# Reordering the matmul groups of an MLP's second projection in a decoder-layer kernel

## The chip, the core and the metric

The kernel runs on one core of one Trainium2 chip. The metric is the device time of one execution in microseconds (us), the median over several runs. Five engines run from separate instruction queues and meet at semaphores: TensorE (PE; its weight loads are listed as PEld), VectorE (DVE), ScalarE (ACT), GpSimd (POOL) and SyncE (SP), which here issues the DMAs from the chip's memory (HBM). The time before is 1776.33 us, the median of 3 runs (1775.65 to 1777.22).

## The reference

One layer of a decoder with 256 tokens and width 2048. Three mixing branches come first; the change touches only the MLP at the end, whose inner width is 8192:

```python
for l in range(DEPTH):
    ...
    x = x + rmsnorm(merged @ w_out[l], g_post_mix[l])
    h2 = rmsnorm(x, g_pre_mlp[l])
    m = jnp.square(jax.nn.relu(h2 @ w_mlp_in[l])) @ w_mlp_out[l]
    x = x + rmsnorm(m, g_post_mlp[l])
return x
```

All data is float32. `w_mlp_in` is 2048 x 8192, `w_mlp_out` 8192 x 2048.

## The kernel before, in words

**Split operands.** Each float32 operand is split into a high part (a cast to fp32r) and a low part (the operand minus the high part), and a product is three matmuls: high by high, high by low, low by high. For a block of weights of 2 x 128 rows by 512 columns (0.5 MB), SP loads it into a buffer `raw`, ACT casts it to `oh`, and DVE subtracts to get `ol`. Six buffers of each kind are used in rotation (`operand`, `raw`). A `raw` buffer can be loaded again when DVE's subtraction has read it; an `oh`/`ol` pair can be written again when PE has used it.

**Stages of the MLP.** The inner width is cut into eight experts `e` of 1024. `mlp_in(e)` makes the first projection in two halves `u` of 512 columns, eight blocks of weights each; at the end of a half, ACT and DVE move the sums out of PSUM into a tile `relu`, DVE squares the positive part in place, and the result is split into `mh` and `ml` (`gen_relu`). `mlp_out(e - 1)` follows `mlp_in(e)` and adds the expert's part of the second projection. `mlp_out_last` does the last expert.

**The second projection.** The output has 2048 columns. Columns 1024 to 2047 are done plainly: for `c` = 2 and 3, `unit` runs over four blocks of weights ("groups", 12 matmuls of 512 columns each) and accumulates two tokens' tiles in PSUM. Columns 0 to 1023 are done by a scheme of seven products instead of eight (`seven`). Products 6, 4, 5 and 3 take sums of blocks of weights, which DVE adds in the `raw` buffers before the split (`summed`); products 0, 1 and 2 take a block as it is (`bare`, the plain products). Each product has two steps `d` = 0 and 1 of 6 matmuls; at the end of `d` = 1 its PSUM bank is added to an accumulator `acc` by DVE (for expert 0, copied by ACT). Products 6 and 4 share one PSUM tile of two banks, and so do 0 and 1. Some products use sums of the activations, which `gen_sums` makes for the next expert: four half-width DVE instructions on `relu`, and two splits `sh`/`sl`. In the order of the program the four steps of the summed products at `d` = 0 come first, then two groups of the unit for `c` = 2, then the summed products at `d` = 1, then the other two groups; the same follows with the plain products and `c` = 3.

**What sets the order.** The code lists work in a program order; the framework that builds the program then places each engine's instructions in an order of its own. Small steps of other work (`gen_sums`, `gen_relu`) are kept in a list `bg`, from which `tick` takes steps after each group or product. In the build before, the squaring and the split of a half go through this list, for the second half only after `drain`.

In the rows below, `mm` is a PSUM tile, and buffer numbers are left out in the profile (so `ol` stands for all six).

Of the kernel before, what the change touches and what calls it, by code (L numbers as in the profile page):

```python
# [10 lines left out]
F32 = mybir.dt.float32  # L11
# [3 lines left out]
ALU = mybir.AluOpType  # L15
AX = mybir.AxisListType

P = 128
D = 2048
S = 256  # L20
NT = S // P
# [12 lines left out]
KG = 2  # L34
# [6 lines left out]
def tile_trunk(ctx: ExitStack, tc, a):  # L41
# [48 lines left out]
    def nm(s):  # L90
        cnt[0] += 1
        return f"{s}_{cnt[0]}"
# [14 lines left out]
    def bank(name):  # L107
        return pbp.tile([P, 512], F32, tag="bp", name=nm(name))
# [52 lines left out]
    bg = []  # L161
# [11 lines left out]
    def drain():  # L173
        while bg:
            pump(1)
# [56 lines left out]
    def unit(act, nk, src, c0, r0=0, order=None, split=False, post=None, ws=None, load=None):  # L232

        if split:
            ps = [bank("mm") for _ in range(2)]
        else:
            both = pmm.tile([P, 1024], F32, tag="mm", name=nm("mm"))  # L240
            ps = [both[:, 0:512], both[:, 512:1024]]
        if order is None:
            order = [(g, None) for g in range(nk // KG)]
        ws = ws or {}
        for i, (g, tt) in enumerate(order):
            k0 = g * KG
            if g not in ws:
                ws[g] = load(src, r0 + k0, c0) if load else load_w(src, r0 + k0, KG, c0)
            wh, wl = ws[g]
            for j in range(KG):  # L250
                kt = k0 + j
                ah, al = act(kt)
                for t in range(NT) if tt is None else (tt,):
                    o = ps[t]
                    st, sl = ah[:, t * P:(t + 1) * P], al[:, t * P:(t + 1) * P]
                    T.matmul(o, st, wh[:, j, :], start=kt == 0, stop=False)
                    T.matmul(o, st, wl[:, j, :], start=False, stop=False)
                    T.matmul(o, sl, wh[:, j, :], start=False, stop=kt == nk - 1)
            tick()
            if post is not None and i + 1 in post:  # L260
                post[i + 1](ps)
        return ps if split else both
# [56 lines left out]
    def act_of(tiles):  # L319
        return lambda kt: (tiles[kt // 4][0][:, kt % 4, :], tiles[kt // 4][1][:, kt % 4, :])  # L320
# [1134 lines left out]
    def raw(src, k0, c0):  # L1455
        w = raws.pop(0)
        raws.append(w)
        nc.sync.dma_start(w, src[k0 * P:(k0 + KG) * P, c0:c0 + 512].rearrange("(k p) n -> p k n", p=P))
        return w
# [24 lines left out]
            yield  # L1484

    def mlp_in(e):
        mt, rs, steps = [], [], []
        for u in range(2):
            c0 = e * 1024 + u * 512
            hi, lo = g4("mh", (P, 4, S), F32R), g4("ml", (P, 4, S), F32R)  # L1490
            r = g4("relu", (P, 4, S))
            if e == 0 and u == 0:
                rt = g4("relut")
                ps = unit(h2act, KT, a["w_mlp_in"][0], c0, order=first, ws=ahead)
                wide_ring()
                A.activation(rt, ps, AF.Relu)
                V.scalar_tensor_tensor(out=rt, in0=ps, scalar=0.0, in1=rt, op0=ALU.max, op1=ALU.mult)
                bg.append(gen_turn(rt, r, hi, lo))
            else:
                if u == 1:  # L1500
                    ps = [bank("mm") for _ in range(4)]
                else:
                    ps = []
                    for _ in range(2):
                        both = pmm.tile([P, 1024], F32, tag="mm", name=nm("mm"))
                        ps.extend((both[:, 0:512], both[:, 512:1024]))
                unit_stacked(h2B, KT, a["w_mlp_in"][0], c0, ps, load_in,
                             {g: ahead[8 + g] for g in range(2)} if e == 0 else {})
                for c in range(4):
                    A.copy(r[:, c, :], ps[c][:, S:2 * S])  # L1510
                    V.tensor_tensor(out=r[:, c, :], in0=ps[c][:, 0:S], in1=r[:, c, :], op=ALU.add)
                steps.append(gen_relu(r, hi, lo))
                if u == 0 or e == 0:
                    bg.append(steps.pop())
            mt.append((hi, lo))
            rs.append(r)
        return mt, rs, steps

    def gen_relu(r, hi, lo):
        V.scalar_tensor_tensor(out=r, in0=r, scalar=0.0, in1=r, op0=ALU.max, op1=ALU.mult)  # L1520
        A.copy(hi, r)
        yield
        V.tensor_tensor(out=lo, in0=r, in1=hi.bitcast(F32), op=ALU.subtract)
        yield

    def gen_sums(rs, ops):

# [20 lines left out]
    def add_w(out, in0, in1):  # L1548
        V.tensor_tensor(out=out, in0=in0, in1=in1, op=ALU.add)
# [3 lines left out]
    def seven(e, mt, ops):  # L1553

        if e == 0:
            for i in range(4):
                t = g4("acc", (P, 2, 512))  # L1560
                accs.extend((t[:, 0, :], t[:, 1, :]))
        acts = [halves_of(mt[0], 0), halves_of(mt[1], 0), halves_of(ops[1], 0), halves_of(mt[1], 1),
                halves_of(ops[0], 1), halves_of(ops[1], 1), halves_of(ops[0], 0)]
        ps = [None] * 7

        def product(i, w, d):
            wh, wl = split_w(w, KG, home=operand)
            for j in range(KG):
                ah, al = [z[:, d * KG + j, :] for z in acts[i]]
                begin, end = d == 0 and j == 0, d == 1 and j == KG - 1  # L1570
                T.matmul(ps[i], ah, wh[:, j, :], start=begin, stop=False)
                T.matmul(ps[i], ah, wl[:, j, :], start=False, stop=False)
                T.matmul(ps[i], al, wh[:, j, :], start=False, stop=end)
            if d == 1:
                if e == 0:
                    A.copy(accs[i], ps[i])
                else:
                    V.tensor_tensor(out=accs[i], in0=ps[i], in1=accs[i], op=ALU.add)
            tick(0.5)

        def summed(d):
            k1 = e * 8 + d * KG
            k2 = k1 + 4
            if d == 0:
                both = pmm.tile([P, 1024], F32, tag="mm", name=nm("mm"))
                ps[6], ps[4] = both[:, 0:512], both[:, 512:1024]
                ps[5], ps[3] = bank("mm"), bank("mm")
            w12, w22, w11, w21 = raw(w_mo, k1, 512), raw(w_mo, k2, 512), raw(w_mo, k1, 0), raw(w_mo, k2, 0)
            add_w(w22, w22, w12)
            add_w(w12, w12, w11)  # L1590
            product(6, w22, d)
            add_w(w11, w22, w11)
            product(4, w12, d)
            add_w(w21, w11, w21)
            product(5, w11, d)
            product(3, w21, d)

        def bare(d):
            k1 = e * 8 + d * KG
            k2 = k1 + 4  # L1600
            if d == 0:
                both = pmm.tile([P, 1024], F32, tag="mm", name=nm("mm"))
                ps[0], ps[1] = both[:, 0:512], both[:, 512:1024]
                ps[2] = bank("mm")
            product(0, raw(w_mo, k1, 0), d)
            product(1, raw(w_mo, k2, 0), d)
            product(2, raw(w_mo, k2, 512), d)

        return summed, bare

    def joined():
# [37 lines left out]

    def mlp_out(e, mt, ops, after):  # L1650
        summed, bare = seven(e, mt, ops)
        for c, part in ((2, summed), (3, bare)):
            if c == 3 and after is not None:
                bg.append(after)
            part(0)
            ps = unit(act_of(mt), 8, w_mo, c * 512, e * 8, split=True, load=load_in, post={2: lambda ps: part(1)})
            if e == 0:
                y_ = g4("yacc", (P, NT, 512))
                yacc[c] = [y_[:, t, :] for t in range(NT)]
            for t in range(NT):  # L1660
                if e == 0:
                    A.copy(yacc[c][t], ps[t])
                else:
                    V.tensor_tensor(out=yacc[c][t], in0=ps[t], in1=yacc[c][t], op=ALU.add)

    def mlp_out_last(e, mt):
        yacc[0:2] = joined()
# [16 lines left out]
                mlp_evac(c, t, ps[t])  # L1684
                gain(c, t)

    prev, rs, _ = mlp_in(0)
    bg.append(gen_s2())
    ops = []
    bg.append(gen_sums(rs, ops))  # L1690
    for e in range(1, NE):
        cur, rs, steps = mlp_in(e)
        drain()
        bg.extend(steps)
        if e == NE - 1:
            gbc = load_gbc(a["g_post_mlp"])
        later = []
        mlp_out(e - 1, prev, ops, gen_sums(rs, later) if e < NE - 1 else None)
        prev, ops = cur, later
    drain()  # L1700
    mlp_out_last(NE - 1, prev)


# [12 lines left out]
```

## Time and profile before

| | before |
|---|---|
| median of 3 runs | 1776.33 us |
| profiled execution | 1776.56 us |
| span from the first to the last instruction | 1774.8 us |
| the MLP's first matmuls to the end | about 1080 to 1775 us of the span |
| granted TensorE clock, mean | 0.999 of full speed |
| DMA | 362.84 MB, 204 GB/s over the span |
| VectorE busy, 1180 to 1696 us | 428.42 of 515.54 us (83%) |

The profiled execution lies 0.23 us above the median. A matmul's end in the profile is modelled, so TensorE counts as busy also where one matmul is followed a little late by the next; starts of successive matmuls show such a delay. The time of a period, from one point of the MLP's loop to the same point in the next, shows it too. Times on the left of a row are starts, in us from the start of the span; behind an arrow stands what released an engine that had waited.

### The profile page before, as it was taken

How to read it: one execution, taken by the hardware profiler on the slowest of the kernel's cores; microseconds unless marked ns; L12 is line 12 of the kernel's file. 1: busy time of each engine (PE TensorE's matmuls, PEld its weight loads, DVE VectorE, ACT ScalarE, POOL GpSimd, SP SyncE). 2: the span in 40 equal slices, each digit the busy share in tenths (PEclk: the TensorE clock that was granted, in tenths of full speed). 3: DMA queues.
4: the chain of work that ended last, by engine and by line, in shares of the span. 5: the costliest groups of instructions: out<-in, count | busy, mean ns of one | idle time of the engine just before them, and what ended most of it. 6: DMA issues, size and time to landing. Idle time of an engine off the chain costs nothing.

```text
span 1774.8 us, 23963 instructions
## 1 busy us (share of the span) xinstructions
PE 1758.9 (99%) x9053; PEld 1491.8 (84%) x9053; DVE 1302.2 (73%) x1764; ACT 961.9 (54%) x1217; POOL 58.0 (3%) x100
## 2 busy tenths in 40 slices
PE   9999999999999999999999999999999999999998
PEld 7888888888888888888888888888888878888886
DVE  5865768685759487798554557786979797979796
ACT  6644666454555475565444445665545454646453
POOL 1000000400030000000000000000000000000000
PEclk9999999999999999999999999999999999999999
DMA  7665555875587465555666765667767676767683
GB/s 268 211 193 167 168 159 164 223 214 157 163 215 206 139 188 167 154 179 167 189 186 189 236 220 198 229 235 237 233 227 250 216 249 216 258 203 250 226 283 142
DMA packets 188804, 362.84 MB, mean 204 GB/s; under 512 B 14456, under 2 KB 16272, under 8 KB 188304
## 3 DMA queue, kind: packets, MB, share of 16 engines
q1 hardware_dynamic: 181856, 351.32, 62.0%
q0 software_dynamic: 2304, 5.44, 1.5%
q10 hardware_dynamic: 4528, 4.54, 0.9%
q8 instruction: 71, 1.16, 0.2%
q14 instruction: 45, 0.37, 0.1%
HBM read 356.86 MB, written 4.39 MB: 204 GB/s over the span
## 4 chain that ended last, share of the span: by engine, by line
PE 77%; DVE 5%; issue 2%; DMA 1%; ACT 0%; DVEq 0%; POOLq 0%; POOL 0%; ACTq 0%
PE mm L56 73%; DVE ol L56 3%; DMA raw<-in_w_mlp_out 1%; PE pa L56 1%; DVE relu L56 1%; DVE raw L56 1%; PE kk L56 0%; DVE ml L56 0%; PE bo L56 0%; PE o L56 0%; PE pzt L56 0%; PE pw L56 0%; PE tr L56 0%; PE y L56 0%; PE mgT L56 0%
## 5 line engine op out<-in xcount | busy, mean ns | idle before, releaser
L56 DVE TENSOR_TENSOR wl<-w,wh 128x1024 fp32r<-128x1024 f32 (+1 forms) x362 | 436.9, 1217 | 236.9 <-ACT wh L56 215.0
L56 ACT CAST wh<-w 128x1024 fp32r<-128x1024 f32 (+1 forms) x362 | 375.7, 1048 | 356.3 <-PE mm L56 301.6
L56 ACT CAST oh<-raw 128x1024 fp32r<-128x1024 f32 x288 | 299.4, 1055 | 270.1 <-PE mm L56 198.9
L56 DVE TENSOR_TENSOR ol<-raw,oh 128x1024 fp32r<-128x1024 f32 x288 | 342.5, 1222 | 93.4 <-ACT oh L56 64.6
L56 PE MATMUL mm<-wh,hh 128*128 128x512 f32 x1152 | 366.2, 392 | 0.0
L56 PEld LDWEIGHTS mm<-wh,hh 128*128 128x128 f32 x1152 | 216.1, 188 | 44.5 <-ACT wh L56 0.3
L56 PE MATMUL mm<-wl,hh 128*128 128x512 f32 x576 | 224.5, 390 | 0.0
L56 PE MATMUL mm<-h2h,oh 128*128 128x512 f32 x960 | 224.4, 390 | 0.0
L56 PEld LDWEIGHTS mm<-h2h,oh 128*128 128x128 f32 x960 | 178.0, 188 | 35.8
L56 PE MATMUL mm<-hh,wh 128*128 128x512 f32 x768 | 184.6, 391 | 0.8 <-ACT z L56 0.8
L56 PEld LDWEIGHTS mm<-hh,wh 128*128 128x128 f32 x768 | 140.6, 188 | 28.3 <-ACT z L56 1.0
L56 PE MATMUL mm<-ol,mh 128*128 128x512 f32 x372 | 145.3, 391 | 2.1 <-DVE ol L56 2.1
L56 PE MATMUL mm<-oh,mh 128*128 128x512 f32 x372 | 145.4, 391 | 0.0
L56 PE MATMUL mm<-oh,ml 128*128 128x512 f32 x372 | 143.8, 389 | 0.0
L56 PEld LDWEIGHTS mm<-wl,hh 128*128 128x128 f32 x576 | 108.2, 188 | 21.2
L56 PEld LDWEIGHTS mm<-h2h,ol 128*128 128x128 f32 x960 | 114.4, 188 | 3.0 <-DVE ol L56 0.7
L56 PE MATMUL mm<-h2h,ol 128*128 128x256 f32 x960 | 115.4, 277 | 0.5 <-DVE ol L56 0.5
L56 PEld LDWEIGHTS mm<-hh,wl 128*128 128x128 f32 x768 | 97.1, 188 | 3.4
L56 PE MATMUL mm<-hh,wl 128*128 128x256 f32 x768 | 99.7, 280 | 0.0
L56 PEld LDWEIGHTS mm<-ol,mh 128*128 128x128 f32 x372 | 69.8, 188 | 18.2 <-DVE ol L56 4.1
L56 PEld LDWEIGHTS mm<-oh,mh 128*128 128x128 f32 x372 | 69.8, 188 | 16.1 <-DVE acc L56 1.6
L56 PEld LDWEIGHTS mm<-oh,ml 128*128 128x128 f32 x372 | 69.8, 188 | 14.4
(363 smaller groups left out, 2209.6 us busy)
## 6 DMA issues: line engine op xcount, KB each, us to landing
w<-in_w_in SPq DMA_DIRECT2D x240, 512.0 KB, 4.2
raw<-in_w_mlp_out SPq DMA_DIRECT2D x170, 512.0 KB, 4.7
raw<-in_w_mlp_in SPq DMA_DIRECT2D x118, 512.0 KB, 4.8
w<-in_w_out SPq DMA_DIRECT2D x32, 512.0 KB, 4.4
w<-in_w_kv_mem SPq DMA_DIRECT2D x30, 512.0 KB, 4.9
w<-in_w_br_c SPq DMA_DIRECT2D x16, 512.0 KB, 3.7
w<-in_w_br_a SPq DMA_DIRECT2D x16, 512.0 KB, 4.4
w<-in_w_br_b SPq DMA_DIRECT2D x16, 512.0 KB, 3.6
```

The lines of the kernel that those rows point to most:

```text
L56: ins = op(*args, **kwargs)
```

## The change

The second projection's program order is turned around. For `c` = 2 and for `c` = 3, a step of a summed product and a group of the unit now follow each other by turns: product 6, group 0, product 4, group 1, product 5, group 2, product 3, group 3. The step `d` = 0 runs with `c` = 2 and `d` = 1 with `c` = 3. The `raw` loads of a step are issued when the step begins, no longer all four ahead. The plain products 0, 1 and 2 follow after both units, each with its two steps in a row. The unit for `c` = 2 accumulates in a two-bank tile, that for `c` = 3 in two single banks. The squaring and its split stand directly behind the evacuation of a half, not in the list `bg`.

```diff
@@ mlp_in
-                steps.append(gen_relu(r, hi, lo))
-                if u == 0 or e == 0:
-                    bg.append(steps.pop())
+                V.scalar_tensor_tensor(out=r, in0=r, scalar=0.0, in1=r, op0=ALU.max, op1=ALU.mult)
+                split_psum(r, hi, lo)
@@ seven
         def summed(d):
             k1 = e * 8 + d * KG
             k2 = k1 + 4
-            ...
-            w12, w22, w11, w21 = raw(w_mo, k1, 512), raw(w_mo, k2, 512), raw(w_mo, k1, 0), raw(w_mo, k2, 0)
+            w12, w22 = raw(w_mo, k1, 512), raw(w_mo, k2, 512)
             add_w(w22, w22, w12)
+            product(6, w22, d)
+            yield
+            w11 = raw(w_mo, k1, 0)
             add_w(w12, w12, w11)
-            product(6, w22, d)
+            product(4, w12, d)
+            yield
             add_w(w11, w22, w11)
-            product(4, w12, d)
+            product(5, w11, d)
+            yield
+            w21 = raw(w_mo, k2, 0)
             add_w(w21, w11, w21)
-            product(5, w11, d)
             product(3, w21, d)
-        def bare(d):
-            ...
+            yield
+        def bare():
+            both = pmm.tile([P, 1024], F32, tag="mm", name=nm("mm"))
+            ps[0], ps[1] = both[:, 0:512], both[:, 512:1024]
+            ps[2] = bank("mm")
+            k1 = e * 8
+            for i, k, c0 in ((0, k1, 0), (1, k1 + 4, 0), (2, k1 + 4, 512)):
+                for d in range(2):
+                    product(i, raw(w_mo, k + d * KG, c0), d)
@@ mlp_out
-        for c, part in ((2, summed), (3, bare)):
+        for c in (2, 3):
             if c == 3 and after is not None:
                 bg.append(after)
-            part(0)
-            ps = unit(act_of(mt), 8, w_mo, c * 512, e * 8, split=True, load=load_in, post={2: lambda ps: part(1)})
+            steps = summed(c - 2)
+            next(steps)
+            ps = unit(act_of(mt), 8, w_mo, c * 512, e * 8, split=c == 3, load=load_in,
+                      post={i: lambda ps: next(steps) for i in (1, 2, 3)})
...
+        bare()
```

Three places in the built programs are used below, all of `mlp_out(2)`, the third of the seven. The first is DVE at the start of the second projection. Before, from the first split behind the evacuation of the `relu` tile (raw3 to raw5 hold blocks that are being summed; raw0 and raw1 hold blocks of the unit's groups):

```order
L56 TENSOR_TENSOR ol1_9548<-raw1_9700,oh1_9547 128x1024
L56 SCALAR_TENSOR_TENSOR relu_1776_11352<-relu_1776_11352 128x1024
L56 TENSOR_TENSOR ol2_9706<-raw3_9702,oh2_9705 128x1024
L56 TENSOR_TENSOR raw4_9703<-raw3_9702,raw4_9703 128x1024
L56 TENSOR_TENSOR ml_1775_11351<-relu_1776_11352,mh_1774_11350 128x1024
L56 TENSOR_TENSOR ol3_9708<-raw2_9701,oh3_9707 128x1024
L56 TENSOR_TENSOR raw5_1690_9704<-raw4_9703,raw5_1690_9704 128x1024
L56 TENSOR_TENSOR ol4_9710<-raw4_9703,oh4_9709 128x1024
L56 TENSOR_TENSOR ol0_9546<-raw0_9549,oh0_9545 128x1024
L56 TENSOR_TENSOR ol5_9712<-raw5_1690_9704,oh5_9711 128x1024
L56 TENSOR_TENSOR acc_1728_10269<-mm_1781_11520,acc_1728_10269 128x512
```

The same place in the changed program:

```order
L56 TENSOR_TENSOR ol1_9548<-raw1_9700,oh1_9547 128x1024
L56 SCALAR_TENSOR_TENSOR relu_1774_11353<-relu_1774_11353 128x1024
L56 TENSOR_TENSOR ol2_9706<-raw2_9701,oh2_9705 128x1024
L56 TENSOR_TENSOR ol3_9708<-raw3_9702,oh3_9707 128x1024
L56 TENSOR_TENSOR ml_1773_11352<-relu_1774_11353,mh_1772_11351 128x1024
L56 TENSOR_TENSOR raw5_1690_9704<-raw5_1690_9704,raw4_9703 128x1024
L56 TENSOR_TENSOR raw4_9703<-raw4_9703,raw1_9700 128x1024
L56 TENSOR_TENSOR ol5_9712<-raw0_9549,oh5_9711 128x1024
L56 TENSOR_TENSOR ol4_9710<-raw5_1690_9704,oh4_9709 128x1024
L56 TENSOR_TENSOR relu_1769_11185<-relu_1769_11185 128x4x128
L56 TENSOR_TENSOR ol0_9546<-raw4_9703,oh0_9545 128x1024
L56 TENSOR_TENSOR ol1_9548<-raw2_9701,oh1_9547 128x1024
```

The squaring (SCALAR_TENSOR_TENSOR) and its split (`ml`) stand where they stood, one row and four rows behind the first split. What moved are the sums of weights (`raw<-raw,raw`) and which blocks the splits serve.

The second place is PE at the end of the second projection. Before, the last group of the unit for `c` = 3 (tiles mm_1788 and mm_1789) is followed by the next expert's first projection (operands `h2h`):

```order
L56 MATMUL mm_1788_11704<-ol5_9712,mh_1749_10726 128x512
L56 MATMUL mm_1788_11704<-oh5_9711,ml_1750_10727 128x512
L56 MATMUL mm_1789_11705<-oh5_9711,mh_1749_10726 128x512
L56 MATMUL mm_1789_11705<-ol5_9712,mh_1749_10726 128x512
L56 MATMUL mm_1789_11705<-oh5_9711,ml_1750_10727 128x512
L56 MATMUL mm_1797_11812<-h2h_1615_9253,oh0_9545 128x512 x4
```

In the changed program the plain products stand there; mm_1789 is the tile that products 0 and 1 share, mm_1790 is product 2, mm_1794 the next first projection:

```order
L56 MATMUL mm_1789_11747<-ol1_9548,mh_1743_10560 128x512
L56 MATMUL mm_1789_11747<-oh1_9547,ml_1744_10561 128x512
L56 MATMUL mm_1790_11748<-oh4_9709,sh_1763_11118 128x512
L56 MATMUL mm_1794_11809<-h2h_1615_9253,oh0_9545 128x512 x4
L56 MATMUL mm_1794_11809<-h2h_1615_9253,oh1_9547 128x512 x2
L56 MATMUL mm_1789_11747<-oh2_9705,mh_1748_10728 128x512
L56 MATMUL mm_1789_11747<-ol2_9706,mh_1748_10728 128x512
L56 MATMUL mm_1789_11747<-oh2_9705,ml_1749_10729 128x512
```

Between product 0 and product 1 stand one matmul of product 2 and six matmuls of the next first projection, on the buffers oh0 and oh1 that product 0 has just used.

The third place is DVE over the same stretch. Before:

```order
L56 TENSOR_TENSOR acc_1726_10267<-mm_1787_11675,acc_1726_10267 128x512
L56 TENSOR_TENSOR sl_1791_11770<-relu_1771_11187,sh_1790_11769 128x1024
L56 TENSOR_TENSOR acc_1725_10266<-mm_1786_11674,acc_1725_10266 128x512
L56 TENSOR_TENSOR sl_1793_11789<-relu_1776_11352,sh_1792_11788 128x1024
L56 TENSOR_TENSOR ol1_9548<-raw1_9700,oh1_9547 128x1024
L56 TENSOR_TENSOR ol2_9706<-raw2_9701,oh2_9705 128x1024
L56 TENSOR_TENSOR yacc_1743_10558<-mm_1788_11704,yacc_1743_10558 128x512
```

In the changed program (ol0 and ol1 serve product 0, ol2 and ol3 product 1):

```order
L56 TENSOR_TENSOR sl_1786_11712<-relu_1769_11185,sh_1785_11711 128x1024
L56 TENSOR_TENSOR ol0_9546<-raw0_9549,oh0_9545 128x1024
L56 TENSOR_TENSOR ol1_9548<-raw1_9700,oh1_9547 128x1024
L56 TENSOR_TENSOR acc_1726_10270<-mm_1781_11523,acc_1726_10270 128x512
L56 TENSOR_TENSOR sl_1788_11727<-relu_1774_11353,sh_1787_11726 128x1024
L56 TENSOR_TENSOR yacc_1740_10498<-mm_1783_11639,yacc_1740_10498 128x512
L56 TENSOR_TENSOR yacc_1740_10498<-mm_1784_11640,yacc_1740_10498 128x512
L56 TENSOR_TENSOR ol2_9706<-raw2_9701,oh2_9705 128x1024
L56 TENSOR_TENSOR ol3_9708<-raw3_9702,oh3_9707 128x1024
L56 TENSOR_TENSOR acc_1725_10269<-mm_1789_11747,acc_1725_10269 128x512
L56 TENSOR_TENSOR ol4_9710<-raw4_9703,oh4_9709 128x1024
```

The row `acc_1725<-mm_1789` empties the bank of product 0, in the tile into which product 1 is to write. It stands behind the two splits of product 1. Before, the evacuations of products 0 and 2 (`acc<-mm_1786`, `acc<-mm_1787`) stood ahead of the unit's last groups.

More of the change, by code (lines that the diff above doesn't have):

```diff
@@ L1486, in mlp_in @@
     def mlp_in(e):
-        mt, rs, steps = [], [], []
+        mt, rs = [], []
         for u in range(2):
@@ L1511, in mlp_in @@
                     V.tensor_tensor(out=r[:, c, :], in0=ps[c][:, 0:S], in1=r[:, c, :], op=ALU.add)
-                steps.append(gen_relu(r, hi, lo))
-                if u == 0 or e == 0:
-                    bg.append(steps.pop())
+                V.scalar_tensor_tensor(out=r, in0=r, scalar=0.0, in1=r, op0=ALU.max, op1=ALU.mult)
+                split_psum(r, hi, lo)
             mt.append((hi, lo))
             rs.append(r)
[L1517 to L1524, printed above, removed]
+        return mt, rs
     def gen_sums(rs, ops):
@@ L1583, in summed @@
             k2 = k1 + 4
[L1584 to L1587, printed above, removed]
-            w12, w22, w11, w21 = raw(w_mo, k1, 512), raw(w_mo, k2, 512), raw(w_mo, k1, 0), raw(w_mo, k2, 0)
+            w12, w22 = raw(w_mo, k1, 512), raw(w_mo, k2, 512)
             add_w(w22, w22, w12)
+            product(6, w22, d)
+            yield
+            w11 = raw(w_mo, k1, 0)
             add_w(w12, w12, w11)
-            product(6, w22, d)
+            product(4, w12, d)
+            yield
             add_w(w11, w22, w11)
-            product(4, w12, d)
+            product(5, w11, d)
+            yield
+            w21 = raw(w_mo, k2, 0)
             add_w(w21, w11, w21)
-            product(5, w11, d)
             product(3, w21, d)
-        def bare(d):
[L1599 to L1607, printed above, removed]
+            yield
[7 more added lines that the diff above has]
+                    product(i, raw(w_mo, k + d * KG, c0), d)
+        both = pmm.tile([P, 1024], F32, tag="mm", name=nm("mm"))
+        ps[6], ps[4] = both[:, 0:512], both[:, 512:1024]
+        ps[5], ps[3] = bank("mm"), bank("mm")
         return summed, bare
@@ L1651, in mlp_out @@
         summed, bare = seven(e, mt, ops)
-        for c, part in ((2, summed), (3, bare)):
+        for c in (2, 3):
             if c == 3 and after is not None:
                 bg.append(after)
-            part(0)
-            ps = unit(act_of(mt), 8, w_mo, c * 512, e * 8, split=True, load=load_in, post={2: lambda ps: part(1)})
+            steps = summed(c - 2)
+            next(steps)
+            ps = unit(act_of(mt), 8, w_mo, c * 512, e * 8, split=c == 3, load=load_in,
+                      post={i: lambda ps: next(steps) for i in (1, 2, 3)})
+            if c == 2:
+                ps = [ps[:, t * 512:(t + 1) * 512] for t in range(NT)]
             if e == 0:
@@ L1685, in mlp_out_last @@
                 gain(c, t)
-    prev, rs, _ = mlp_in(0)
+    prev, rs = mlp_in(0)
     bg.append(gen_s2())
@@ L1691, in tile_trunk @@
     for e in range(1, NE):
-        cur, rs, steps = mlp_in(e)
+        cur, rs = mlp_in(e)
         drain()
-        bg.extend(steps)
         if e == NE - 1:
@@ L1699, in tile_trunk @@
         prev, ops = cur, later
-    drain()
     mlp_out_last(NE - 1, prev)
```

## The prediction

> **What bounds the kernel now.** I read the totals first, then the MLP by periods of its loop, then TensorE's waits, then single rows around one wait.
>
> ```profile
> PE 1758.9 (99%) x9053; PEld 1491.8 (84%) x9053; DVE 1302.2 (73%) x1764; ACT 961.9 (54%) x1217; POOL 58.0 (3%) x100
> ```
>
> TensorE is the bound nearly everywhere, so a reordering can only give back what TensorE still waits. Each row below is one period, from a point behind the wait in one second projection to the same point in the next: length, then busy time of PE, PEld, DVE, ACT, POOL, granted clock, DMA.
>
> ```profile
> 1180.41:1267.10 86.69, 86.28 (x442) 73.44 (x442) 67.91 (x67) 50.86 (x62) 0.00 (x0) 1.00 0.71 239
> 1267.10:1353.07 85.97, 85.35 (x436) 72.15 (x436) 71.95 (x76) 45.67 (x51) 0.00 (x0) 1.00 0.70 232
> 1353.07:1439.17 86.10, 85.46 (x436) 72.08 (x436) 72.02 (x76) 45.22 (x51) 0.00 (x0) 1.00 0.70 233
> 1439.17:1524.20 85.03, 85.03 (x436) 72.24 (x436) 71.90 (x76) 45.78 (x51) 0.00 (x0) 1.00 0.70 235
> 1524.20:1609.86 85.66, 85.21 (x438) 72.23 (x437) 72.12 (x77) 45.11 (x51) 0.00 (x0) 1.00 0.71 234
> 1609.86:1695.95 86.09, 85.57 (x439) 72.61 (x439) 72.53 (x77) 44.84 (x50) 0.00 (x0) 1.00 0.75 247
> ```
>
> The fourth period has no wait: 85.03 us is the floor. DVE is busy 72 of these 85 us, so it is the next engine. The waits themselves, over all periods, and the two that end worst (the rows give a matmul's start and modelled length):
>
> ```profile
> PE mm L56 <- DVE ol L56: 3.2, 5, 1.1
> PE mm L56 <- DVE acc L56: 0.5, 1, 0.5
> ```
>
> ```profile
> 1178.90 0.39 PE L56 MATMUL mm<-oh,sh 128*128 128x512 f32 x1
> 1180.41 0.50 PE L56 MATMUL mm<-ol,sh 128*128 128x512 f32 x1 [1.13 <-DVE ol L56]
> ...
> 1338.27 0.39 PE L56 MATMUL mm<-oh,sh 128*128 128x512 f32 x1
> ...
> 1349.83 0.39 PE L56 MATMUL mm<-oh,sh 128*128 128x512 f32 x1
> 1350.06 0.39 PE L56 MATMUL mm<-ol,sh 128*128 128x512 f32 x1
> ...
> 1352.07 0.39 PE L56 MATMUL mm<-oh,mh 128*128 128x512 f32 x1
> 1353.07 0.50 PE L56 MATMUL mm<-ol,mh 128*128 128x512 f32 x1 [0.62 <-DVE ol L56]
> ```
>
> From 1338.27 to 1350.06 stand 52 undisturbed steps: 0.227 us a matmul, so 1.36 us for a step of a product (6) and 2.72 us for a group (12). The wait at 1180 is 1.51 - 0.23 = 1.28 us, that at 1353 1.00 - 0.23 = 0.77 us. All lie about 15 us behind the start of a second projection, and DVE's split ends them.
>
> **Why DVE is late there.** DVE's queue around that start:
>
> ```profile
> 1332.17 2.36 DVE L56 TENSOR_TENSOR ol<-raw,oh 128x1024 fp32r<-128x1024 f32 x2 [1.14 <-PE mm L56]
> 1334.83 1.23 DVE L56 TENSOR_TENSOR raw<-raw,raw 128x1024 f32<-128x1024 f32 x1 [0.30 <-DMA raw<-in_w_mlp_out]
> 1337.98 1.23 DVE L56 TENSOR_TENSOR raw<-raw,raw 128x1024 f32<-128x1024 f32 x1 [1.92 <-DMA raw<-in_w_mlp_out]
> 1339.12 1.22 DVE L56 TENSOR_TENSOR ol<-raw,oh 128x1024 fp32r<-128x1024 f32 x1
> 1340.26 1.41 DVE L56 TENSOR_TENSOR relu<-mm,relu 128x256 f32<-128x256 f32 x4
> 1341.58 1.22 DVE L56 TENSOR_TENSOR ol<-raw,oh 128x1024 fp32r<-128x1024 f32 x1
> 1342.71 1.22 DVE L56 SCALAR_TENSOR_TENSOR relu<-relu 128x1024 f32<-128x1024 f32 x1
> ...
> 1349.52 3.50 DVE L56 TENSOR_TENSOR ol<-raw,oh 128x1024 fp32r<-128x1024 f32 x3
> 1352.93 1.29 DVE L56 TENSOR_TENSOR acc<-mm,acc 128x512 f32<-128x512 f32 x2
> 1354.12 1.22 DVE L56 TENSOR_TENSOR ol<-raw,oh 128x1024 fp32r<-128x1024 f32 x1
> ```
>
> Start to start, a full-width instruction takes 3.41 / 3 = 1.14 us, a half-width one 1.19 / 2 = 0.60 us, the four evacuations of `relu` 1.32 us. A summed step costs DVE a sum and a split, 2.27 us, against 1.36 us of TensorE; a group costs it 1.14 us against 2.72 us. Before, four summed steps come in a row (9.1 us of DVE against 5.4), and DVE's lead is spent.
>
> **First part: the turns.** A summed step and a group together cost DVE 3.4 us and TensorE 4.1 us, so DVE gains on TensorE. I walk DVE's new queue of this period with these paces. Ahead of 1338 nothing that matters differs: both orders wait for a block loaded into a buffer that a split frees (the first of the two that begin at 1332.17, so at about 1333.3).
>
> ```profile
> raw<-in_w_mlp_out SPq DMA_DIRECT2D x170, 512.0 KB, 4.7
> raw<-in_w_mlp_in SPq DMA_DIRECT2D x118, 512.0 KB, 4.8
> ```
>
> 1333.3 + 4.7 = 1338.0, which is when the row at 1337.98 starts. From there: sum and split for product 5, the evacuations, then the rows of the new order up to the split for product 6 at `d` = 1, which ends at 1351.8. TensorE needs it after four steps and four groups, 1338.27 + 4 x 4.08 = 1354.6: a margin of 2.8 us where the old order lacked 0.8. These waits go. Their sum is 1.28 us (at 1180) plus the excess of the periods over 85.03 us (0.94, 1.07, 0.63, 1.06), and for the first period only its length less PE's busy time, 0.41, because I can't place the rest: **-5.4 us**. Bounds: 3.7 us (the listed waits) and 6.6 us (that period's full excess of 1.66).
>
> **Second part: the plain products last.** They cost 1.14 us of DVE per 1.36 us of TensorE, but the new second projection leaves DVE no slack before them: from 1338.0 to the split of product 0 it has to do all summed steps, the squaring, eight groups' splits, the evacuations and the sums of activations, back to back. By the walk the splits of product 0 end at 1368.5 and 1369.6, those of product 1 at 1373.7 and 1374.8, and product 0's bank is emptied at 1375.4. TensorE gets through the turns and product 0 by 1338.27 + 156 x 0.227 = 1373.7. Product 1 writes the tile from which DVE empties product 0, and such a write waits for the whole tile:
>
> ```profile
> 1353.67 0.19 PEld L56 LDWEIGHTS mm<-oh,sh 128*128 128x128 f32 x1 [0.30 <-DVE acc L56]
> ```
>
> Here product 4 starts as soon as product 6's bank, the other one of its tile, has been emptied. So product 1 can't start before 1375.4. Seven matmuls stand in between, six of them on blocks reloaded into buffers that product 0's splits free: 1368.5 + 4.8 (DMA) + 1.06 (cast) = 1374.4 for the first, 1375.5 for the second.
>
> ```profile
> L56 ACT CAST oh<-raw 128x1024 fp32r<-128x1024 f32 x38 | 39.7, 1054 | 37.2 <-PE mm L56 26.4 <-DMA raw<-in_w_mlp_out 5.4 <-DVE raw L56 3.7
> ```
>
> TensorE then stands at 1376.0 where it could have been at 1373.7 + 7 x 0.227 = 1375.3: 0.7 us lost. A reload of 512 KB is the step that decides. The Trainium skill, page "DMA: Bandwidth & Descriptors", section "Anatomy of one DMA — SWDGE (gpsimd) path", fits a DMA's time (for the other path) by 2.0 us plus the bytes over 436 GB/s, an estimate of 3.2 us for this block; by it the reload would be hidden, 0.1 us be left of the 0.7, and the whole come out at 1774.4 - 5 x 0.6 = 1771.4 us. The rows say 4.7 and 4.8 us, and the sum goes by them.
>
> The same walk for the second and the next three second projections, whose rows differ a little, gives 0.1, 0.9, 0.75 and 0.1 us. A walk leaves out every unevenness, and these only add, so I take 0.7 us for each of the five middle ones: **+3.5 us**. Bounds: 0, and 2.2 us each (11 us) if the reload takes 1.5 us more than the median, well within what single loads took:
>
> ```profile
> DMA to landing us min/median/max: 3.5/4.8/7.6
> ```
> The first and the last are spared: in the first, ACT evacuates the accumulators; in the last, the sums of activations are missing (four half-width and two full-width instructions, 4.7 us of DVE).
>
> **Third part: the squaring.** It stands at the same place of DVE's queue, so I cost it at nothing. Its cover is the evacuation and the split ahead of it; moved ahead of that split it would delay it by 1.14 us against a lead of over 3 us. The c = 2 unit's other tile and the DMAs' order move no byte more; SP issues in the order in which DVE frees the buffers, with none blocked that I found. The end after the last matmul is unchanged.
>
> **Sum.** Against the profiled execution (span 1774.8 plus 1.76 outside): 1776.56 - 5.4 + 3.5 = 1774.7; it ran 0.23 above the median, so 1774.4 us.
>
> **The rivals.**
> - *The tail costs nothing.* If DVE has a little more lead than walked (the load that both orders wait for at 1338 landing 1 us earlier is enough), all of the first part stays: 1776.33 - 5.4 = 1770.9. For it: two of the five walks are near 0. Against it: DVE's queue is full for 37 us.
> - *The tail becomes the bound.* The wait of product 1 for product 0's bank, with the reloads ahead of it in TensorE's queue, takes the place of the wait removed. From 5.4 / 5 = 1.1 us per middle second projection the change is slower; at 2.2 us it gives 1776.33 - 5.4 + 11 = 1781.9. For it: the fixed order on TensorE makes it wait for two reloads although product 1's operands lie ready.
> - *The turns don't do what they should.* Both orders hang on the same load at 1338; if the sums, now spread, meet a later load, the old waits stay and the tail comes on top: 1776.33 + 3.5 = 1779.8. Against it: the margin of 2.8 us.
>
> **How the numbers follow.** Forecast 0.5, first rival 0.2, second 0.2, third 0.1. A difference of 0.2%, 3.55 us, is about what a measurement of this kernel can tell from none. The forecast (-2 us) and the third rival (+3.5) lie within it, so: faster 0.2, within 0.2% 0.6, slower 0.2. The range goes from the first rival, 1770.8, to between the last two, 1780.5.
>
> **What would show it.** Right: no wait of TensorE for a split 10 to 17 us after a second projection's start; instead waits at its end, for `acc` or a reloaded `oh`, in the middle five, under 1.2 us each; periods near 85.7. Wrong: waits within the turns, periods of 85.0 (tail free) or above 86.2 (tail bound), or a first or last second projection with a wait of its own. The weakest number is the tail's 0.7 us, a difference of two sums of some 40 us.

## The result, and the profile after

| | before | after |
|---|---|---|
| median, six runs each on one chip | 1776.76 us (1775.65 to 1777.30) | 1786.64 us (1784.83 to 1788.59) |
| ratio to before | | 1.0057, 95% interval 1.0044 to 1.0070 |
| span of the profiled execution | 1774.8 us | 1786.6 us |

The change makes the kernel slower, by 9.9 us (the spans of the two profiled executions differ by 11.8; the profiled one after lies 1.7 us above its median). The totals of the page hide it: TensorE's busy time counts also where a matmul is followed late.

```profile
PE 1762.0 (99%) x9053; PEld 1493.0 (84%) x9053; DVE 1300.4 (73%) x1764; ACT 959.9 (54%) x1217; POOL 57.9 (3%) x100
```

The periods show it. These rows run from the first matmul of one second projection to that of the next (columns as in the prediction's table). Each holds the same work, 436 matmuls; the counts take in one or two on the edges:

```profile
1165.33:1252.38 87.05, 85.44 (x437) 72.23 (x436) 66.14 (x64) 50.04 (x63) 0.00 (x0) 1.00 0.70 230
1252.38:1340.31 87.93, 85.45 (x438) 72.16 (x437) 71.80 (x76) 45.35 (x52) 0.00 (x0) 1.00 0.70 228
1340.31:1426.77 86.46, 85.37 (x437) 72.22 (x436) 71.40 (x76) 45.68 (x52) 0.00 (x0) 1.00 0.69 230
1426.77:1514.90 88.13, 85.73 (x437) 72.16 (x436) 71.65 (x75) 45.55 (x52) 0.00 (x0) 1.00 0.69 227
1514.90:1602.27 87.37, 85.50 (x438) 72.16 (x437) 71.61 (x76) 45.38 (x52) 0.00 (x0) 1.00 0.69 229
1602.27:1689.05 86.78, 85.38 (x438) 72.24 (x437) 71.73 (x76) 45.36 (x52) 0.00 (x0) 1.00 0.70 231
```

What such a period takes without waits shows in one of the runs below, which has the change's order and a seventh `raw` buffer; its five middle periods take 84.56 to 84.62 us, the first of them:

```profile
1252.35:1336.96 84.61, 84.61 (x437) 72.40 (x436) 71.81 (x76) 45.68 (x52) 0.00 (x0) 1.00 0.72 236
```

Over 84.6 us stand 2.5 us in the changed kernel's first period and 3.3, 1.9, 3.5, 2.8 and 2.2 us in the five middle ones, 13.7 us together. From the start of the last of the seven second projections (1689.05) to the end it takes 97.6 us, against 93.1 in the run with seven buffers, so 4.5 us more. What TensorE waited for in the MLP after 1160 us (engine, tile, releaser: total, times, longest):

```profile
PE mm L56 <- ACT oh L56: 4.6, 6, 1.3
PE mm L56 <- DVE acc L56: 4.6, 6, 1.4
PE mm L56 <- DVE ol L56: 1.8, 3, 0.7
PE mm L56 <- ACT acc L56: 1.4, 1, 1.4
```

The old waits for splits (`ol`, 3.2 us) lay some 15 us behind a second projection's start; none is left there. The new ones, for casts of reloaded blocks (`oh`) and for emptied banks (`acc`), lie mostly at its end, and some inside the turns. TensorE's rows of the third second projection, which starts at 1340.31, show both:

```profile
1361.19 0.47 PE L56 MATMUL mm<-oh,sh 128*128 128x512 f32 x1 [0.33 <-DVE acc L56]
...
1376.24 0.39 PE L56 MATMUL mm<-oh,sh 128*128 128x512 f32 x1
1376.88 1.20 PE L56 MATMUL mm<-h2h,oh 128*128 128x512 f32 x4 [0.25 <-ACT oh L56]
1378.58 0.73 PE L56 MATMUL mm<-h2h,oh 128*128 128x512 f32 x2 [0.51 <-ACT oh L56]
1379.15 0.40 PE L56 MATMUL mm<-oh,mh 128*128 128x512 f32 x1
```

At 1361.19 product 4 waits for product 6's bank, in the middle of the turns. At 1376 the seven matmuls stand that the prediction named: one of product 2, then four and two of the next first projection, each group late, then product 1. The chain of work that ends with them (start, length, what):

```profile
1349.36 1.23 DVE raw L56
...
1356.90 1.23 DVE raw L56
...
1358.14 5.03 DMA raw<-in_w_mlp_out
...
1363.27 1.06 ACT oh L56
...
1364.36 1.23 DVE ol L56
...
1370.85 2.28 DVE ol L56 x2
...
1373.15 4.23 DMA raw<-in_w_mlp_in
...
1377.48 1.06 ACT oh L56
...
1378.58 3.46 PE mm L56 x14
```

Read from the second row: DVE sums two blocks of weights at 1356.90; only then can a buffer be reloaded, and that load takes 5.03 us; the cast and DVE's split of the block follow at once. The program's rows on DVE at this place say which buffer:

```
L56 TENSOR_TENSOR raw5_1690_9704<-raw5_1690_9704,raw4_9703 128x1024
...
L56 TENSOR_TENSOR raw1_9700<-raw5_1690_9704,raw1_9700 128x1024
...
L56 TENSOR_TENSOR ol5_9712<-raw5_1690_9704,oh5_9711 128x1024
```

raw5 holds `w22`, which is summed for product 6 and is still needed for the sum of product 5, two turns later. The block that waits for raw5 is one of the unit's groups. By the program's order and at TensorE's pace (an estimate), a sum's block stays in its `raw` buffer for two turns, 8.2 us (4.08 each); in a row it was two steps, 2.7 us. DVE's own rows don't bear that out as a longer hold: from the sum for product 6 to that for product 5 they have 7.5 us here (1349.36 to 1356.90) and 10.2 us before (1334.83 to 1344.98), where DVE waits for a load in between. So two readings stood against each other after the result: the **tail** (product 1 has to wait for product 0's bank, wherever the lateness comes from) and the **ring** (six `raw` buffers are too few for the time for which this order holds them, so loads start late and everything behind them is late).

### The profile page after: what moved, and what is told of

It is laid out like the page before. It is cut to its first block, busy times and chain, and to the rows that moved or that the text cites. A ratio compares the mean times of both kernels' runs of the same rounds, so it can differ in the third digit from the quotient of the medians.

```text
span 1786.6 us, 23922 instructions
## 1 busy us (share of the span) xinstructions
PE 1762.0 (99%) x9053; PEld 1493.0 (84%) x9053; DVE 1300.4 (73%) x1764; ACT 959.9 (54%) x1217; POOL 57.9 (3%) x100
## 4 chain that ended last, share of the span: by engine, by line
PE 66%; DVE 10%; DMA 5%; issue 3%; ACT 1%; DVEq 0%; POOLq 0%; POOL 0%; ACTq 0%
PE mm L56 62%; DMA raw<-in_w_mlp_out 5%; DVE ol L56 5%; DVE relu L56 2%; DVE raw L56 2%; PE pa L56 1%; ACT oh L56 1%; DVE acc L56 1%; DMA raw<-in_w_mlp_in 1%; PE kk L56 0%; DVE sl L56 0%; DVE yacc L56 0%; PE bo L56 0%; PE o L56 0%; PE pzt L56 0%
## 5 line engine op out<-in xcount | busy, mean ns | idle before, releaser
L56 DVE TENSOR_TENSOR raw<-raw,raw 128x1024 f32<-128x1024 f32 x56 | 68.4, 1221 | 29.1 <-DMA raw<-in_w_mlp_out 28.6
```

What stands on the lines that cost most here:

```text
L56: ins = op(*args, **kwargs)
```

## The experiments

Each time is a median on the chip on which the kernel before was run beside it; the chips differ, so the ratios to the kernel before are what compares.

**Product 1 in a bank of its own.** Product 2 takes its place in product 0's tile.

```diff
-            ps[0], ps[1] = both[:, 0:512], both[:, 512:1024]
-            ps[2] = bank("mm")
+            ps[0], ps[2] = both[:, 0:512], both[:, 512:1024]
+            ps[1] = bank("mm")
```

> The changed kernel, but product 1 accumulates in a bank of its own and product 2 shares product 0's tile. Theory T (the tail: product 1 waits until DVE has emptied product 0's bank, and six matmuls on reloaded blocks stand ahead of it): TensorE's waits for acc (3.3 + 1.4 us listed) and for oh (4.6 us listed) at the second projections' ends go, and of the 21 us by which matmuls start late over the MLP about 15 go: 1770 to 1775 us. Rival L (loads: the sums taken by turns hold raw buffers longer, so loads come late and DVE is late as a whole): the wait only moves to product 1's or 2's split, 1783 to 1787 us. Rival Q (the squaring's place): no change, 1786 us.

Measured: 1784.68 us against 1776.71, ratio 1.0038 (1.0023 to 1.0053). TensorE's waits in this kernel:

```profile
PE mm L56 <- DVE acc L56: 3.9, 5, 1.4
PE mm L56 <- DVE ol L56: 3.2, 6, 1.0
PE mm L56 <- ACT acc L56: 2.0, 2, 1.2
```

The coupling through the tile is gone, but the time has hardly moved (the ratio's interval meets that of the changed kernel, 1.0044 to 1.0070): the waits went over to splits, and to product 4's tile inside the turns. By this run the tail is where the lateness shows, not where it comes from.

**The squaring deferred again**, in the changed kernel.

```diff
-                V.scalar_tensor_tensor(out=r, in0=r, scalar=0.0, in1=r, op0=ALU.max, op1=ALU.mult)
-                split_psum(r, hi, lo)
+                steps.append(gen_relu(r, hi, lo))
+                if u == 0 or e == 0:
+                    bg.append(steps.pop())
```

> The changed kernel, with the squaring and its split put back into the list of background steps. Theory T and rival L: no change, 1785 to 1788 us. Rival Q (the squaring, done at once, delays the splits behind it): back to the time before or faster, 1771 to 1777 us.

Measured: 1788.96 us, ratio 1.0070 (1.0053 to 1.0087). Not faster than the changed kernel: the squaring's place isn't the cause.

**The plain products last, and nothing else**, in the kernel before.

```diff
-            part(0)
-            ps = unit(act_of(mt), 8, w_mo, c * 512, e * 8, split=True, load=load_in, post={2: lambda ps: part(1)})
+            if c == 2:
+                summed(0)
+            ps = unit(act_of(mt), 8, w_mo, c * 512, e * 8, split=True, load=load_in, post={2: lambda ps: summed(1)} if c == 2 else None)
...
+        bare()
```

> The kernel before, with one part of the change: the plain products last (summed products and groups as before, in a row; squaring deferred as before). Theory T: the old waits stay and the tail's come on top, 1776.8 + 10 to 15 us: 1786 to 1792 us. Rival L: without the sums by turns the loads come as before; near the time before, 1775 to 1780 us.

Measured: 1777.38 us, ratio 1.0004 (0.9995 to 1.0013). The plain products at the end cost nothing by themselves, against the tail theory.

**Finer turns, and nothing else**, in the kernel before: two summed steps and a group by turns with `c` = 2, and, not shown below, plain products and groups by turns with `c` = 3.

```diff
+            for d in range(2):
...
+                w12, w22 = raw(w_mo, k1, 512), raw(w_mo, k2, 512)
+                add_w(w22, w22, w12)
+                product(6, w22, d)
+                w11 = raw(w_mo, k1, 0)
+                add_w(w12, w12, w11)
+                product(4, w12, d)
+                yield
+                add_w(w11, w22, w11)
+                product(5, w11, d)
+                w21 = raw(w_mo, k2, 0)
+                add_w(w21, w11, w21)
+                product(3, w21, d)
+                yield
...
-            ps = unit(act_of(mt), 8, w_mo, c * 512, e * 8, split=True, load=load_in, post={2: lambda ps: part(1)})
+            steps = part()
+            next(steps)
+            ps = unit(act_of(mt), 8, w_mo, c * 512, e * 8, split=True, load=load_in, post={i: lambda ps: next(steps) for i in (1, 2, 3)})
```

> The kernel before, with finer turns alone: two steps of summed products and one group by turns with c = 2, plain products and groups by turns with c = 3, which ends with a group; sums take their loads when the step begins; squaring deferred as before. Theory T (turns are sound, the tail is what costs): the waits 15 us after a second projection's start shrink and nothing comes at its end, 1770 to 1775 us. Rival L (loads issued late cost): 1780 us or more.

Measured: 1770.35 us, ratio 0.9963 (0.9948 to 0.9977), faster than before. After 1160 us the profile lists no wait of TensorE at all. Here a group follows every two summed steps, so at TensorE's pace `w22` is held for 5.4 us (two steps of 1.36 and a group of 2.72), not 8.2. Turns as such are sound; what is different in the change is either their kind (the hold) or what stands at the end.

**The sums of activations later.** At this point I suspected DVE's own load: that it arrives at the plain products without a lead.

```diff
-            if c == 3 and after is not None:
-                bg.append(after)
...
         bare()
+        if after is not None:
+            bg.append(after)
```

> The changed kernel, with the sums of activations (four half-width instructions and two splits, 4.7 us of DVE) moved from the turns of c = 3 to behind the plain products, into the next first projection. Theory D (DVE arrives at the plain products without lead, because its whole work of the second projection stands ahead of them): TensorE's waits at the second projections' ends nearly go, 1771 to 1777 us. Rival R (the ring of six raw buffers: sums by turns hold three of them, so loads land late): the loads are as late as before, 1783 to 1787 us.

Measured: 1792.36 us, ratio 1.0089 (1.0074 to 1.0104). That theory missed, with the wrong sign: 4.7 us less of DVE's work ahead of the tail didn't help.

```profile
PE mm L56 <- DVE acc L56: 7.6, 7, 1.2
PE mm L56 <- DVE ol L56: 5.8, 9, 0.8
```

In this kernel the framework put eight matmuls of product 2 ahead of product 1, and they wait for their splits. It is 5.7 us slower than the changed kernel. Part of that is TensorE's clock: in this profile it is at half for 3.41 us twice (from 1557.94 and from 1646.68), in the changed kernel once, and one such stretch cost about 1.6 us there (last section). The rest wasn't tried apart.

**A seventh `raw` buffer.**

```diff
-        raws.append(g4("raw5", (P, KG, 512)))
+        raws.extend(g4(f"raw{i}", (P, KG, 512)) for i in (5, 6))
```

> The changed kernel with a seventh raw buffer. Rival R: DVE's waits for loads (28.6 us listed over the MLP's second projections) fall to half or less and with them TensorE's at the ends, 1772 to 1778 us. Theory D: little, 1782 to 1787 us.

Measured: 1781.80 us, ratio 1.0032 (1.0020 to 1.0044), between the two theories. The trace says why. In the second projections TensorE waits for nothing any more, but there is one new stall far ahead of them, in the second first projection, with a slow clock in it:

```profile
1132.54 6.09 PE L56 MATMUL mm<-h2h,oh 128*128 128x512 f32 x16 [9.93 <-ACT oh L56]
```

By the code the seventh buffer is a tile from the activations' pool. That the pool has none to spare at that moment is inferred; a later run, in which the tile is taken after this place, has no such stall.

**The four loads ahead again**, which holds the buffers longer.

```diff
-            w12, w22 = raw(w_mo, k1, 512), raw(w_mo, k2, 512)
+            w12, w22, w11, w21 = raw(w_mo, k1, 512), raw(w_mo, k2, 512), raw(w_mo, k1, 0), raw(w_mo, k2, 0)
...
-            w11 = raw(w_mo, k1, 0)
...
-            w21 = raw(w_mo, k2, 0)
```

> The changed kernel, with the four loads of a summed step issued together at its beginning, as in the kernel before, so that w11 and w21 hold their buffers two and four turns longer. Rival R: slower by 5 us or more, 1791 us and above. Theory D: within 2 us of the changed kernel, 1785 to 1789 us.

Measured: 1796.29 us, ratio 1.0121 (1.0100 to 1.0142). In the code nothing was changed but when `w11` and `w21` take their `raw` buffers, and the loss doubles, to 19.9 us over the kernel before on its chip (1796.29 - 1776.43). TensorE's waits for casts go from 4.6 to 7.0 us:

```profile
PE mm L56 <- ACT oh L56: 7.0, 5, 3.1
```

**Two summed steps and a group by turns, then the unit of `c` = 3, then the plain products last.**

```diff
+            if c == 2:
+                steps = summed()
+                next(steps)
+            ps = unit(act_of(mt), 8, w_mo, c * 512, e * 8, split=True, load=load_in, post={i: lambda ps: next(steps) for i in (1, 2, 3)} if c == 2 else None)
...
         bare()
```

> The turns of the fastest run so far (two summed steps and one group by turns, all with c = 2), then the unit of c = 3 by itself, then the plain products last; squaring at once. Theory D: the four groups of c = 3 (2.72 us of TensorE for 1.14 of DVE) give DVE its lead back ahead of the plain products; 1770 to 1773 us. Rival T (a wait for product 0's bank and the reloaded blocks whatever stands ahead): 1778 us or more. Rival R: 1770 to 1775 us as well, the sums' buffers being held shorter.

Measured: 1770.64 us, ratio 0.9967 (0.9955 to 0.9979). The plain products stand where the change puts them, the squaring is done at once, and the kernel is as fast as with finer turns alone. It differs from the change in the kind of turns, in the groups of `c` = 3 ahead of the plain products, and in two single banks for the unit of `c` = 2; the next run keeps all of the change's order.

**The seventh buffer, joining late.**

```diff
         cur, rs = mlp_in(e)
         drain()
+        if e == 1:
+            raws.append(g4("raw6", (P, KG, 512)))
```

> The changed kernel with a seventh raw buffer that joins only after the second first projection, so that the single 10 us stall that the seventh buffer brought there (its tile came from the pool of the activations) doesn't come. Rival R: no wait of TensorE is left in the second projections, 1768 to 1773 us, the same as the turns with shorter held sums. Theory D or T: 1780 us or more.

Measured: 1770.25 us against 1777.00, ratio 0.9962 (0.9948 to 0.9976). Its only listed wait of TensorE after 1160 us, and ACT's and DVE's waits for loads:

```profile
PE mm L56 <- DVE ol L56: 0.8, 1, 0.8
...
ACT oh L56 <- DMA raw<-in_w_mlp_out: 7.3, 3, 3.4
ACT oh L56 <- DMA raw<-in_w_mlp_in: 0.7, 1, 0.7
...
DVE raw L56 <- DMA raw<-in_w_mlp_out: 25.7, 19, 3.1
```

The same waits in the changed kernel:

```profile
ACT oh L56 <- DMA raw<-in_w_mlp_out: 42.3, 18, 5.1
ACT oh L56 <- DMA raw<-in_w_mlp_in: 25.7, 29, 2.6
...
DVE raw L56 <- DMA raw<-in_w_mlp_out: 28.6, 10, 4.1
```

With one buffer more and nothing else, ACT's 68 us of waiting for loads become 8, and the chain of work over the stretch that is shown above is a single row:

```profile
1339.85 42.19 PE mm L56 x188
```

DVE's own waits for loads stay (25.7 us of 28.6) without a cost in time; in the changed kernel most of them lie around a second projection's start, such as 3.5 us ahead of 1340.08. What went with the lost time are the casts' waits for loads.

**The seventh buffer in the kernel before** (the same lines).

> The kernel before with the same seventh raw buffer. If the ring of raw buffers also set the old waits (DVE waits about 1.9 us for the load of a fourth sum at each start): 1769 to 1773 us. If they came from four sums in a row alone, that is DVE's own pace: 1775 to 1777 us.

Measured: 1777.57 us, ratio 1.0005 (0.9995 to 1.0014).

```profile
PE mm L56 <- DVE acc L56: 3.6, 5, 0.9
```

TensorE still waits some 14 us behind a second projection's start, now for a bank that DVE empties instead of for a split. So the old waits were not the ring's to give back. DVE's waits for loads are still there (27.0 us listed), so that its own pace in four sums in a row is all of it isn't shown by this run alone; the finer turns, with six buffers, took the waits away.

**The plain products first**, with the change's turns behind them.

```diff
         summed, bare = seven(e, mt, ops)
+        bare()
...
-        bare()
```

> The changed kernel with the plain products ahead of the two units instead of behind them; turns of one summed step and one group as in the change. Theory T (last is what costs): 1769 to 1775 us. Rival R (the sums' buffers are held as long as before): waits within the turns, 1779 us or more.

Measured: 1817.92 us, ratio 1.0227 (1.0212 to 1.0243).

```profile
PE mm L56 <- ACT oh L56: 23.0, 18, 3.1
```

Without the plain products at the end it is far slower, and the waits for casts lie within the turns. So with six buffers the turns of one step and one group starve here too, with nothing behind them. Why this order loses so much more than the change was not taken apart: the framework also mixed its steps more finely, and in this profile TensorE's clock is at half for 17 us (four stretches), which by halving alone would be some 8 of the 41 us lost (an estimate).

**The squaring at once, and nothing else**, in the kernel before: the lines of the second experiment's diff, with signs exchanged.

> The kernel before with the third part of the change alone: squaring and split directly behind the evacuation. All theories that are left (the ring of raw buffers under the turns): no change, 1775 to 1779 us. Rival Q (the squaring's place costs): 1781 us or more.

Measured: 1776.04 us against 1777.06, ratio 0.9993 (0.9983 to 1.0003): no change.

## Why the prediction was wrong, step by step

**The bound** (TensorE) was right: two kernels with hardly a wait left come out at 1770.25 and 1770.35 us, with spans of 1768.4 and 1768.5. The floor of 85.03 us a period was 0.4 us too high, since the changed order with seven buffers takes 84.6. In the period without a listed wait, three matmuls (at 1439.51, 1440.11 and 1460.46) still start 0.33 to 0.34 us behind the one before instead of 0.227.

**The first part, the turns, -5.4 us,** was right in mechanism and 1 us short in size. Where nothing takes it back, finer turns give 1776.71 - 1770.35 = 6.4 us, within the bounds of 3.7 to 6.6, and the change's own turns with seven buffers 1777.00 - 1770.25 = 6.8 us. What the step left out are waits inside the turns, above all for product 6's bank (1361.19 and its like): in the five middle second projections the late starts there come to 3.2 us. (The sum at 1338.0, which the walk gives to product 5, is by the order in which the sums use each other product 3's; its price is the same.)

**The second part, the plain products last, +3.5 us.** The place and the order of events were right: seven matmuls, two reloads, product 1 behind them. (Seven in the third second projection; four to seven in the five middle ones.) The size was not: by the start of product 1 the five middle ones are 13.3 us late, from the starts of their matmuls at 0.227 us each. The 3.2 us inside the turns taken off, some 10 us are left at the end, 2.0 us each, just under the upper bound of 2.2. In the third second projection everything starts 2.04 us later than in the walk (1340.31 for 1338.27), so product 0's splits were due at 1369.6 + 2.04 = 1371.6; they end at 1373.1. Most of the difference is DVE's idle time ahead of the split at 1364.36:

```profile
1364.36 1.23 DVE L56 TENSOR_TENSOR ol<-raw,oh 128x1024 fp32r<-128x1024 f32 x1 [1.04 <-ACT oh L56]
```

**The step that failed** is the walk itself: DVE was walked "back to back" from 1338.0 on, with each block taken as loaded when DVE's queue came to it. The third part dismissed the loads in one sentence ("SP issues in the order in which DVE frees the buffers, with none blocked that I found"). That order was true, but between 1338.0 and the tail the walk has no load that comes late, and in the changed kernel ACT's casts wait 68 us for loads after 1160 us. One buffer more takes the whole loss away (1786.64 to 1770.25 us), taking two of the buffers earlier doubles it (1796.29). So the ring of six `raw` buffers is what this order runs short of; that a sum's block is held longer by the turns is the likely reason, argued from the program's order and not shown by DVE's rows. With the loads in time, product 1's wait for the shared tile costs nothing: in the run with the late seventh buffer products 0 and 1 share their tile as in the change.

**"The first and the last are spared"** was wrong. In the first, product 1 waits for ACT, whose evacuation of product 0 comes too late:

```profile
1202.48 0.39 PE L56 MATMUL mm<-oh,sh 128*128 128x512 f32 x1
1204.24 0.50 PE L56 MATMUL mm<-oh,mh 128*128 128x512 f32 x1 [1.38 <-ACT acc L56]
```

Less the 0.227 us of a step, 1.53 us are lost here. ACT's copies stand in the same queue as the casts. But this is not the ring's price: the run with seven buffers reaches its second second projection no earlier (1252.35 against 1252.38), with a wait of 0.8 us for a split in the first. In the last second projection product 1 starts 2.9 us late, and 1.6 us more go through the slow clock below, 4.5 together.

**The cited formula** of the Trainium skill, page "DMA: Bandwidth & Descriptors", section "Anatomy of one DMA — SWDGE (gpsimd) path" (an estimate of 3.2 us a block for the other path, 1771.4 us in all), doesn't describe these loads: the two in the chain took 5.03 and 4.23 us.

**The third part, the squaring, at nothing,** was right (ratio 0.9993, with 1 inside its interval).

**The sum** with the measured sizes, as spans: the change's order with its loads in time gives 1768.4 - 1774.8 = -6.4 us. Against that run the changed kernel loses nothing up to the start of the second second projection, 13.7 us over the five middle ones (1252.38 to 1689.05, against 1252.35 to 1675.30), and 4.5 us behind: -6.4 + 13.7 + 4.5 = +11.8 us, which is the difference of the spans.

**The rivals.** "The tail becomes the bound" was the nearest: its place and its sign came true, and its price for the middle five (11 us) nearly (some 10 us at the end). Its cause did not: a bank of its own for product 1 left 1784.68 us. "The turns don't do what they should", if the sums "meet a later load", had the cause in half a sentence, but priced it as the old waits coming back, and the margin of 2.8 us that spoke against it was walked without loads.

## What to carry to other kernels

When an order is changed, walk the rings of buffers and not only the engines: note for each buffer when its last reader comes, and add load and cast behind it. Spreading dependent sums among other work evens out the engine that makes them, but it also changes when each buffer of the ring comes free; here a ring that was just large enough then starved work that has nothing to do with the sums. Two cures came out equal here, another kind of turns (two steps and a group, 1770.35 us) and one buffer more (1770.25 us); their ratios to the kernel before are 0.9963 (0.9948 to 0.9977) and 0.9962 (0.9948 to 0.9976).

## What was not expected of the hardware

Behind a short run of waits TensorE's clock was at half for 3.4 us. In the last second projection of the changed kernel:

```profile
1726.29 0.39 PE L56 MATMUL mm<-oh,sh 128*128 128x512 f32 x1
1727.35 0.50 PE L56 MATMUL mm<-ol,sh 128*128 128x512 f32 x1 [0.68 <-DVE ol L56]
1729.09 0.50 PE L56 MATMUL mm<-oh,mh 128*128 128x512 f32 x1 [1.24 <-DVE acc L56]
...
1730.12 0.62 PE L56 MATMUL mm<-ol,mh 128*128 128x512 f32 x1
1730.54 0.63 PE L56 MATMUL mm<-oh,ml 128*128 128x512 f32 x1
```

The stretch that begins there has a granted clock of 0.50 (third number from the end):

```profile
1730.11:1733.53 3.42, 3.42 (x10) 2.64 (x8) 2.41 (x4) 1.99 (x2) 0.00 (x0) 0.50 0.89 329
```

From 1730.12 on eight matmuls start 0.43 us apart instead of 0.227, 1.6 us lost. Ahead of it stand 2.8 us (1726.29 to 1729.09) with one matmul in between and no listed wait over 1.24 us. The Trainium skill, page "TensorE: Matmul & The Clock Gate", section "Why this matters for your kernels", warns of idle gaps of more than about 3 us; the gaps here were shorter. That they brought the slow clock is likely and not shown. Such stretches of 3.41 us at 0.50 stand in other runs too, in that with the sums later and in that with four loads ahead (from 1555.46). But it doesn't happen each time: from 1288.07 on TensorE started four matmuls in 3.8 us, with the clock at 1.00 in that whole period.

```profile
1288.07 0.39 PE L56 MATMUL mm<-oh,sh 128*128 128x512 f32 x1
1289.50 0.96 PE L56 MATMUL mm<-h2h,oh 128*128 128x512 f32 x3 [1.04 <-ACT oh L56]
1291.86 0.50 PE L56 MATMUL mm<-oh,mh 128*128 128x512 f32 x1 [1.39 <-DVE acc L56]
```
